# Strassen projections of a two-layer encoder: results held in PSUM, halves of q and k paired, weight sums on GpSimd

## The chip, the cores and the metric

The kernel runs on one core of one Trainium2 chip. Five engines share its SBUF: TensorE (PE, matrix products into PSUM, with PEld for its weight loads), VectorE (DVE), ScalarE (ACT), GpSimd (POOL) and SyncE (SP, which issues nearly all DMAs from one queue in order). The metric is the time of one execution on the device, in microseconds, of the slowest core, here the only one.

## The reference, cut to what matters

The trunk has two layers over a sequence of 2048 positions of width 1024. Layer 0 is a short gated convolution. Layer 1 is a dilated sliding-window attention with 8 heads of 128 and three groups (windows 128, 512, 2048 at rates 1, 4, 16). The change concerns the input projection of layer 1 and the rotation of q and k:

```python
h, gate = adaln_pre_norm(x, c, norm_g[i], w_mod[i], b_mod[i])     # (1, 2048, 1024)
q, k, v, z = jnp.split(h @ w_in, [G * E, 2 * G * E, 2 * G * E + E], axis=-1)   # 3072, 3072, 1024, 1024 columns
q = apply_rope(q.reshape(B, S, G, H, Dh), cos, sin)
k = apply_rope(k.reshape(B, S, G, H, Dh), cos, sin)

def apply_rope(x, cos, sin):
    x1, x2 = jnp.split(x.astype(jnp.float32), 2, axis=-1)
    return jnp.concatenate([x1 * cos - x2 * sin, x2 * cos + x1 * sin], axis=-1)
```

Behind it come banded attention in each group, a softmax over the three groups, `* silu(z)`, the output projection, the residual and a final RMSNorm.

## The kernel before, in words

All of it is one function, `build`, that issues instructions into pools of tiles; a scheduler then sets the order of each engine from the data's dependences and the pools' free buffers. Activations lie transposed: a tile holds 128 features by 512 positions (`CH`); the sequence has four such chunks (`NCH`).

Float32 products are made of three products of a reduced format: each operand is cut into a high and a low part (`cut`, `split`), and `hi*hi + hi*lo + lo*hi` is summed in PSUM.

Layer 0 ends with its output projection for chunks 2 and 3, which writes the residual stream `x1_d` and, between its matmuls, makes forms of the first half (`make_forms`, called with `c == 2`). `SumSq` gathers the sum of squares of a chunk for the norm; `ss.rstd()` sums over partitions with a matmul on PE into `ss` (L211) and takes the root (L152 to L157); the result goes to `r_d`.

The projections of layer 1 are the stretch that the change is about. They use Strassen's scheme (in Winograd's form) one level deep. The sequence is handled in two halves of two chunks each; the inner dimension is halved into k tiles 0 to 3 and 4 to 7; and two blocks of 128 output columns are one pair (`pair`). Seven products take the place of eight. The forms of the activations (`FN`: "11", "T2", "T3", "T1", "21", "22", "T4") are made once per half and lie in SBUF as `F`; the first four are in pool `fa`, the others in `fb`. The forms of the weights (`w_forms`) are made for every pair: two raw tiles `wraw` (512 KB each) are loaded, S1, S2, S3 and S4 (A12 - S2) are computed into tiles `st`, then each of the seven is cast on ACT (L529) and its low part subtracted (L425, in `sub`) into a tile `wf`, of which there are eight. A product (`prod`, L537) is 12 matmuls of 128 by 512; a pair is 84.

A half has 32 pairs (`jobs`): 4 for z, 4 for v, 24 for q and k, in this order. In a q/k pair the one block is the q and the other the k of a head and group. `pair` sums the products into four tiles `u` in SBUF (L541, L559) and hands each to `emit`:

- z: SiLU on ACT, then a store.
- v: four transposes on PE (L585), a copy out of PSUM, a store.
- q and k (`qk_out`): ACT copies the two 64-partition halves crosswise into `sw` (L603, L604), DVE multiplies by cos (L605), POOL multiplies `sw` by sin (L606), DVE adds both into `R`, in an order of positions that suits the group's rate (L607), and two stores go to `q_d` and `k_d` (L612).

At the turn between the halves (last pair of the first, first pair of the second) `pair` runs with `by_k`: it goes over the k tiles outside and the seven products inside, so that a k tile's forms can be replaced as soon as it is done (`load_forms`, through a ring of six tiles `fs`). The forms of the second half are made behind the pairs 8, 12, 16 and 20 of the first (the q/k pairs begin with 8) and kept in DRAM.

Behind the projections come the pools of the attention (`mk`, `qkp`), whose loads of q and k (`load_qk`, L668) stand on SP behind the last stores of `R`.

## Time and profile before

| what | us |
|---|---|
| median of 3 runs (lowest, highest) | 3091.41 (3088.41, 3094.56) |
| the profiled execution's own time | 3090.82 |
| its span, first to last instruction | 3089.0 |
| PE busy | 2816.2 |
| DVE busy | 2032.4 |
| POOL busy | 1410.9 |
| ACT busy | 1208.9 |

The engines run beside each other, so busy times don't add up to the span. [...] In the slices of the page PE and its clock are below their full marks from about 950 us to 1200 us, and again and again until 2450.

### The profile page before, as it was taken

Reading aid. Unit: us, or ns where it says so; the run is one execution under the profiler, and the core shown is the slowest. Engines: PE = TensorE matmul, PEld = TensorE weight load, DVE = VectorE, ACT = ScalarE, POOL = GpSimd, SP = SyncE. Lnnn points to the kernel's source line nnn. Section 1 sums busy time; section 2 is a strip of 40 time slices with the busy share of each in tenths; the row PEclk is TensorE's granted clock in tenths of the full one; section 3 lists DMA queues with packets and bytes.
Section 4 is the critical chain, followed back from the end, with each engine's and each line's share of the span. In section 5 each row is a group of like instructions: output and inputs, shape, how many; then the busy total and the mean of one; then the engine's idle time right before and its main releaser. Section 6 shows DMA issues by size and latency. Waiting matters only on the chain. (4 is left out here: it accounts for less than half of the span.)

```text
span 3089.0 us, 39549 instructions
## 1 busy us (share of the span) xinstructions
PE 2816.2 (91%) x13910; PEld 2372.2 (77%) x13910; DVE 2032.4 (66%) x3265; ACT 1208.9 (39%) x2599; POOL 1410.9 (46%) x1038
## 2 busy tenths in 40 slices
PE   5999997999997969998989699998989689999998
PEld 4999995888886758877777487877777578887888
...
GB/s 217 67 80 69 74 118 118 87 70 81 68 130 167 181 195 112 96 95 96 90 96 95 156 122 98 89 102 90 96 96 95 133 211 235 219 219 196 173 155 96
DMA packets 246694, 384.66 MB, mean 125 GB/s; under 512 B 89056, under 2 KB 146656, under 8 KB 238304
## 3 DMA queue, kind: packets, MB, share of 16 engines
...
## 5 line engine op out<-in xcount | busy, mean ns | idle before, releaser
L537 PE MATMUL mm<-fT,wf 128*128 128x512 f32 x3072 | 770.9, 407 | 105.4 <-DVE u L541 85.8
L537 PEld LDWEIGHTS mm<-fT,wf 128*128 128x128 f32 x3072 | 600.5, 197 | 257.0 <-ACT wf L529 112.5
L537 PE MATMUL mm<-f,wf 128*128 128x512 f32 x2304 | 561.3, 394 | 16.3 <-ACT u L559 6.9
L537 PEld LDWEIGHTS mm<-f,wf 128*128 128x128 f32 x2304 | 435.2, 190 | 109.8 <-ACT u L559 7.3
L127 POOL TENSOR_TENSOR wf<-wraw,wf 128x512 fp32r<-128x512 f32 x148 | 198.1, 1340 | 591.1 <-ACT wf L126 586.2
L606 POOL TENSOR_TENSOR sw<-sw,sin 128x512 f32<-128x512 f32 x192 | 348.7, 1816 | 162.8 <-ACT sw L604 162.8
L135 PE MATMUL mm<-hA,wf 128*128 128x342 f32 (+1 forms) x2304 | 369.8, 323 | 6.0 <-DVE hA L225 5.6
L135 PEld LDWEIGHTS mm<-hA,wf 128*128 128x128 f32 x2304 | 366.8, 191 | 7.6 <-DVE hA L225 6.5
L607 DVE TENSOR_TENSOR R<-u,sw 128x512 f32<-128x512 f32 x192 | 322.3, 1678 | 66.2 <-POOL sw L606 62.2
L135 PE MATMUL mm<-hB,wf 128*128 128x512 f32 x1536 | 351.6, 391 | 0.0
L135 PEld LDWEIGHTS mm<-hB,wf 128*128 128x128 f32 x1536 | 288.8, 188 | 61.4 <-issue 1.5
L425 POOL TENSOR_TENSOR wf<-st,wf 128x512 fp32r<-128x512 f32 x192 | 249.8, 1313 | 152.5 <-ACT wf L529 152.5
L541 DVE TENSOR_TENSOR u<-mm,u 128x512 f32<-128x512 f32 x384 | 256.8, 685 | 89.1 <-PE mm L537 72.9
L529 ACT CAST wf<-st 128x512 fp32r<-128x512 f32 x256 | 148.1, 618 | 335.9 <-DVE st L425 308.4
L605 DVE TENSOR_TENSOR u<-u,cos 128x512 f32<-128x512 f32 x192 | 233.0, 1214 | 67.3 <-ACT sw L604 67.3
L603 ACT COPY sw<-u 64x512 f32<-64x512 f32 x192 | 118.9, 619 | 324.5 <-DVE u L541 318.7
L811 PE MATMUL po<-ptS,v 128*128 128x128 f32 (+1 forms) x1280 | 199.0, 288 | 21.0 <-ACT ptS L794 8.4
L425 POOL TENSOR_TENSOR wf<-wraw,wf 128x512 fp32r<-128x512 f32 x128 | 170.5, 1332 | 85.1 <-ACT wf L529 83.8
L811 PEld LDWEIGHTS po<-ptS,v 128*128 128x128 f32 (+1 forms) x1280 | 165.4, 192 | 47.2 <-ACT ptS L794 13.3
L696 ACT ACTIVATE pr<-pr,stat 128x256 f32<-128x256 f32 (+2 forms) x384 | 173.6, 454 | 69.7 <-DVE stat L694 68.6
L692 PE MATMUL pq<-k,q 128*128 128x256 f32 (+2 forms) x768 | 169.0, 349 | 33.7 <-DMA k<-k_d 33.7
L135 PE MATMUL mm<-y,wf 128*128 128x512 f32 x768 | 180.4, 397 | 0.0
...
## 6 DMA issues: line engine op xcount, KB each, us to landing
...
```

What stands on the lines that cost most here:

```text
L127: e.tensor_tensor(out=t[:, 1], in0=part, in1=t[:, 0].bitcast(F32), op=ALU.subtract)
L135: PE.matmul(ps, lhs(l, kt), rhs(r, kt), start=start and i == 0 and j == 0, stop=stop and i == n - 1 and j == 2)
L425: eng.tensor_tensor(out=out, in0=in0, in1=in1, op=ALU.subtract)
L529: SC.copy(out=t[:, 0], in_=x)
L537: PE.matmul(ps, W[i][:, l, k, :], F[FN[i]][:, r, k, :], start=k == 0 and j == 0, stop=k == HK - 1 and j == 2)
L541: V.tensor_tensor(out=out, in0=in0, in1=in1, op=op)
L605: V.tensor_tensor(out=src, in0=src, in1=cos[:, cs], op=ALU.mult)
L606: G.tensor_tensor(out=sw, in0=sw, in1=sin[:, cs], op=ALU.mult)
L607: V.tensor_tensor(out=Rs[m].rearrange("p (r j) -> p j r", r=r)[:, t * n:(t + 1) * n, :], in0=src.rearrange("p (j r) -> p j r", r=r), in1=s ...
L692: PE.matmul(pq[:, j, 0:n], q[:, q0:q0 + P], k[:, k0:k0 + n], start=True, stop=True)
L696: SC.activation(out=pr[:, j, 0:n], in_=pr[:, j, 0:n], func=AF.Exp, scale=-1.0, bias=m_ap, accum_out=l_ap)
L811: PE.matmul(po[:, b % 4, :], vt[0:m, vc, :], ptS[0:m, i, :], start=ci == 0, stop=ci == len(parts) - 1)
```

## The change

The arithmetic of the seven products stays. What changes around them:

- **Blocks.** The columns of the q and k weights are put in another order on the host: a pair's first block holds the first 64 dimensions of q and of k, its second block the second 64 of both. `cos` and `sin` have the same values in both halves of the partitions. A rotation is then `A cos - B sin` and `B cos + A sin` of the two blocks, with no crossing of partitions; the crosswise copies and POOL's products go. A tile `R` now holds halves of q and k, and is stored with four DMAs of 64 partitions.
- **PSUM.** Four of the seven products become the results, in place: adds write the bank that they read. `u` is left for three partial sums x, y, z. DVE multiplies by sin into a tile `t` and by cos in place in PSUM, and the `R` sums read PSUM. z's SiLU reads PSUM; v is first copied to SBUF by ACT.
- **Weights.** All sums and low parts are on POOL, with their tiles `st` in a pool of their own (`stp`) that is there before the stage. `w_forms` of the next pair is issued before `pair` of this one.
- **Order and pools.** The first half runs z, q/k, v; the second z, v, q/k. The forms of the second half are made behind pairs 1 to 4. The sums of squares of chunks 2 and 3 are stored as they are (`r_d`), and the root is taken behind pair 0. The ring for forms (six tiles) and the two rows `r23` lie in q and k tiles of the attention's first buffer (`qk0`), which is there from the start of the stage; the second buffer is `qk1`.

```diff
+    stp = tc.alloc_tile_pool(name="stp", bufs=1, side="right")
...
-        ss = SumSq(op, CH)
+        ss = SumSq(op, CH, row=False)
...
-        SY.dma_start(out=r_d[c], in_=ss.rstd())
+        V.tensor_tensor(out=ss.acc, in0=ss.acc, in1=ss.sq, op=ALU.add)
+        SY.dma_start(out=r_d[c], in_=ss.acc)
...
+    qk0 = tc.alloc_tile_pool(name="qk0", bufs=1)
+    spare = [t[:, i * CH:(i + 1) * CH] for t in [qk0.tile([P, S], F32, name=n) for n in ("q", "k")] for i in range(4)]
+    r23 = spare[:2]
+    fring = itertools.cycle(spare[2:])
...
-        S1, S2, S3 = (l1.tile([P, HK, P], F32, name="st", bufs=4) for i in range(3))
+        S1, S2, S3 = (stp.tile([P, HK, P], F32, name="st", bufs=4) for i in range(3))
         G.tensor_tensor(out=S1, in0=A21, in1=A22, op=ALU.add)
-        sub(S2, S1, A11, V)
+        sub(S2, S1, A11, G)
...
-        for x, eng in ((A11, G), (S2, V), (S3, G), (S1, G), (A12, G), (None, G), (A22, V)):
+        for x, eng in ((A11, G), (S2, G), (S3, G), (S1, G), (A12, G), (None, G), (A22, G)):
...
-                sub(x, A12, S2, V)
+                sub(x, A12, S2, G)
...
-        SC.copy(out=c11, in_=product(0))
-        add(c12, product(1), c11)
-        add(c21, product(2), c12)
-        p5 = product(3)
-        add(c12, p5, c12)
-        add(c22, p5, c21)
+        p1 = product(0)
+        x, y, z = (l1.tile([P, CH], F32, name="u", bufs=4) for i in range(3))
+        SC.copy(out=x, in_=p1)
+        add(y, product(1), x)
+        add(z, product(2), y)
+        c22 = product(3)
+        add(y, c22, y)
+        add(c22, c22, z)
         emit(1, 1, c22)
-        add(c11, product(4), c11)
+        c11 = product(4)
+        add(c11, c11, x)
         emit(0, 0, c11)
-        add(c12, product(5), c12)
+        c12 = product(5)
+        add(c12, c12, y)
         emit(0, 1, c12)
-        add(c21, c21, product(6), ALU.subtract)
+        c21 = product(6)
+        add(c21, z, c21, ALU.subtract)
         emit(1, 0, c21)
...
         def emit(m, t, src):
-            cs = slice(t * CH, (t + 1) * CH)
-            sw = l1.tile([P, CH], F32, name="sw", bufs=2)
-            SC.copy(out=sw[0:64], in_=src[64:128])
-            SC.copy(out=sw[64:128], in_=src[0:64])
-            V.tensor_tensor(out=src, in0=src, in1=cos[:, cs], op=ALU.mult)
-            G.tensor_tensor(out=sw, in0=sw, in1=sin[:, cs], op=ALU.mult)
-            V.tensor_tensor(out=Rs[m].rearrange("p (r j) -> p j r", r=r)[:, t * n:(t + 1) * n, :],
-                            in0=src.rearrange("p (j r) -> p j r", r=r),
-                            in1=sw.rearrange("p (j r) -> p j r", r=r), op=ALU.add)
...
+            s_ = t_tile()
+            mul(s_, src, sin, t)
+            mul(src, src, cos, t)
+            got[m, t] = src, s_
+            if (1 - m, t) not in got:
+                return
+            done.append(t)
+            for i in range(2):
+                V.tensor_tensor(out=Rs[i].rearrange("p (r j) -> p j r", r=r)[:, t * n:(t + 1) * n, :],
+                                in0=got[i, t][0].rearrange("p (j r) -> p j r", r=r),
+                                in1=got[1 - i, t][1].rearrange("p (j r) -> p j r", r=r),
+                                op=ALU.add if i else ALU.subtract)
...
+    jobs = [(half, *j) for half in range(2) for j in ((zj + qj + vj) if half == 0 else (zj + vj + qj))]
...
+    Wn = w_forms(*jobs[0][1:3])
+    load_forms(0)
+    for i, (half, s0, s1, what, args) in enumerate(jobs):
+        W = Wn
+        if i + 1 < len(jobs):
+            Wn = w_forms(*jobs[i + 1][1:3])
+        if i == NJ:
+            load_forms(1)
...
+        pair(W, what(half, *args), i in (NJ - 1, NJ))
...
+        if 1 <= i <= 4:
+            make_forms(lambda: next(fring), 1, i - 1, r23, store_form(1))
...
-            qk[hd, g] = [qkp.tile([P, S], F32, name=n) for n in ("q", "k")]
+            qk[hd, g] = [(qk1 if (hd * NG + g) % 2 else qk0).tile([P, S], F32, name=n) for n in ("q", "k")]
```

The scheduler moves work at three places that matter here. The names in the rows are those of the tiles; a line of the kernel after stands some lines later than before.

First, DVE in a q/k pair. Before, from the end of one pair into the next (`u` and `R` in SBUF, `sw` from POOL, `st`, `wraw` and `wf` the weights):

```order
L607 TENSOR_TENSOR R1_11332<-u_11335,sw_11455 128x512
L425 TENSOR_TENSOR st_11631<-st_11630,wraw_11626 128x512
L425 TENSOR_TENSOR st_11651<-wraw_11626,st_11631 128x512
L425 TENSOR_TENSOR wf_11639<-st_11631,wf_11639 128x512
L541 TENSOR_TENSOR u_11498<-mm_11515,u_11497 128x512
L541 TENSOR_TENSOR u_11499<-mm_11529,u_11498 128x512
L541 TENSOR_TENSOR u_11498<-mm_11543,u_11498 128x512
L541 TENSOR_TENSOR u_11500<-mm_11543,u_11499 128x512
L605 TENSOR_TENSOR u_11500<-u_11500,cos_8071 128x512
L541 TENSOR_TENSOR u_11497<-mm_11564,u_11497 128x512
L607 TENSOR_TENSOR R1_11496<-u_11500,sw_11558 128x128x4
L605 TENSOR_TENSOR u_11497<-u_11497,cos_8071 128x512
```

After, from a pair's first add on (`mm` is a PSUM bank, `t` the product with sin):

```order
L544 TENSOR_TENSOR u_10891<-mm_10894,u_10890 128x512
L544 TENSOR_TENSOR u_10892<-mm_10908,u_10891 128x512
L544 TENSOR_TENSOR u_10891<-mm_10922,u_10891 128x512
L544 TENSOR_TENSOR mm_10922<-mm_10922,u_10892 128x512
L612 TENSOR_TENSOR t_10937<-mm_10922,sin_7403 128x512
L612 TENSOR_TENSOR mm_10922<-mm_10922,cos_7402 128x512
L544 TENSOR_TENSOR mm_10940<-mm_10940,u_10890 128x512
L612 TENSOR_TENSOR t_10954<-mm_10940,sin_7403 128x512
L612 TENSOR_TENSOR mm_10940<-mm_10940,cos_7402 128x512
L544 TENSOR_TENSOR mm_10957<-mm_10957,u_10891 128x512
L612 TENSOR_TENSOR t_10971<-mm_10957,sin_7403 128x512
L612 TENSOR_TENSOR mm_10957<-mm_10957,cos_7402 128x512
```

The weight operations have left DVE, a result is written back to its bank, and each product follows its add directly, without `sw` between.

Second, POOL at the start of the projections (`f_7408` and `f_7396` are the form "21", `fT` is a form with T in its name; `q` and `k` in the rows after are tiles of the ring). Before, from the first pair's sums on:

```order
L520 TENSOR_TENSOR st<-wraw 128x512
L425 TENSOR_TENSOR st<-wraw 128x512
L425 TENSOR_TENSOR wf<-st,wf 128x512 x2
L425 TENSOR_TENSOR wf<-wraw,wf 128x512
L425 TENSOR_TENSOR wf<-st,wf 128x512
L425 TENSOR_TENSOR f_7408<-fs,f_7408 128x512 x4
L425 TENSOR_TENSOR wf<-wraw,wf 128x512
L425 TENSOR_TENSOR fT_7410<-fs,fT_7410 128x512 x4
L520 TENSOR_TENSOR st<-wraw 128x512
```

After, from the second pair's sums on:

```order
L523 TENSOR_TENSOR st<-wraw 128x512
L426 TENSOR_TENSOR st<-st,wraw 128x512
L426 TENSOR_TENSOR st<-wraw 128x512
L426 TENSOR_TENSOR st<-wraw,st 128x512
L426 TENSOR_TENSOR f_7396<-q,f_7396 128x512
L426 TENSOR_TENSOR wf<-st,wf 128x512
L426 TENSOR_TENSOR f_7396<-q,f_7396 128x512
L426 TENSOR_TENSOR wf<-st,wf 128x512
L426 TENSOR_TENSOR f_7396<-k,f_7396 128x512 x2
L426 TENSOR_TENSOR wf<-st,wf 128x512
L426 TENSOR_TENSOR fT_7398<-k,fT_7398 128x512
L426 TENSOR_TENSOR wf<-wraw,wf 128x512
```

The four sums of the second pair's weights, and two low parts, now stand ahead of or between the cuts of "21"; before, four cuts of "21" followed the low parts of the first pair's weights.

Third, POOL at the turn between the halves. Before, from a sum for the second half's first pair on:

```order
L425 TENSOR_TENSOR st<-wraw 128x512
L425 TENSOR_TENSOR f_7408<-fs,f_7408 128x512
L425 TENSOR_TENSOR fT_7410<-fs,fT_7410 128x512
L425 TENSOR_TENSOR f_6619<-fs,f_6619 128x512
L425 TENSOR_TENSOR fT_6621<-fs,fT_6621 128x512
L425 TENSOR_TENSOR f_7408<-fs,f_7408 128x512
L425 TENSOR_TENSOR fT_7410<-fs,fT_7410 128x512
L425 TENSOR_TENSOR f_6619<-fs,f_6619 128x512
L425 TENSOR_TENSOR wf<-st,wf 128x512 x2
L425 TENSOR_TENSOR wf<-wraw,wf 128x512
```

After, from the last sum for that pair on:

```order
L426 TENSOR_TENSOR st<-wraw,st 128x512
L426 TENSOR_TENSOR fT_6624<-k,fT_6624 128x512
L426 TENSOR_TENSOR f_7396<-q,f_7396 128x512
L426 TENSOR_TENSOR fT_7398<-k,fT_7398 128x512
L426 TENSOR_TENSOR f_6622<-k,f_6622 128x512
L426 TENSOR_TENSOR fT_6624<-k,fT_6624 128x512
L426 TENSOR_TENSOR f_7396<-q,f_7396 128x512
L426 TENSOR_TENSOR fT_7398<-k,fT_7398 128x512
L426 TENSOR_TENSOR f_6622<-k,f_6622 128x512
L426 TENSOR_TENSOR fT_6624<-q,fT_6624 128x512
L426 TENSOR_TENSOR f_7396<-k,f_7396 128x512
L426 TENSOR_TENSOR wf<-st,wf 128x512 x3
```

Six low parts of the weights stand behind the cuts of forms, as before; there are ten cuts between the last sum and the first of these low parts, and no sums of others.

## Rows read from the trace of the kernel before

**Rows 1.** part 1 of the page: busy us, share of the span, instructions of each engine
```profile
PE 2816.2 (91%) x13910; PEld 2372.2 (77%) x13910; DVE 2032.4 (66%) x3265; ACT 1208.9 (39%) x2599; POOL 1410.9 (46%) x1038
```

**Rows 2.** stretches: length, busy PE, PEld, DVE, ACT, POOL, PEclk, DMA share, GB/s
```profile
992.50:1209.00 216.50, 177.28 (x746) 138.79 (x745) 117.50 (x135) 73.76 (x126) 105.00 (x80) 0.91 0.53 166
1209.00:1701.80 492.80, 455.53 (x1926) 370.07 (x1925) 421.45 (x419) 211.99 (x354) 378.39 (x244) 0.97 0.30 94
1701.80:1781.30 79.50, 54.11 (x182) 38.56 (x181) 67.07 (x61) 40.07 (x70) 64.96 (x43) 0.81 0.48 146
1781.30:1924.40 143.10, 143.10 (x653) 115.39 (x652) 58.72 (x77) 50.46 (x85) 66.16 (x52) 1.00 0.38 116
1924.40:2438.10 513.70, 475.38 (x2005) 385.58 (x2003) 439.54 (x439) 220.74 (x368) 388.76 (x252) 0.97 0.29 92
```

**Rows 3.** timeline of PE, second half: start, us, engine, line, instruction, count
```profile
1781.29 8.32 PE L537 MATMUL mm<-fT,wf 128*128 128x512 f32 x36
...
1800.33 8.32 PE L537 MATMUL mm<-fT,wf 128*128 128x512 f32 x36
...
1859.93 8.33 PE L537 MATMUL mm<-fT,wf 128*128 128x512 f32 x36
...
1881.39 8.33 PE L537 MATMUL mm<-fT,wf 128*128 128x512 f32 x36
```

**Rows 4.** groups, second q/k stretch: line, count | busy us, mean ns | idle before
```profile
L606 POOL TENSOR_TENSOR sw<-sw,sin 128x512 f32<-128x512 f32 x92 | 167.2, 1818 | 77.1 <-ACT sw L604 77.1
...
L607 DVE TENSOR_TENSOR R<-u,sw 128x512 f32<-128x512 f32 x92 | 153.9, 1673 | 31.8 <-POOL sw L606 29.9
L605 DVE TENSOR_TENSOR u<-u,cos 128x512 f32<-128x512 f32 x92 | 112.2, 1220 | 32.9 <-ACT sw L604 32.9
L541 DVE TENSOR_TENSOR u<-mm,u 128x512 f32<-128x512 f32 x140 | 93.9, 685 | 8.5 <-PE mm L537 3.8
L425 POOL TENSOR_TENSOR wf<-st,wf 128x512 fp32r<-128x512 f32 x69 | 88.0, 1288 | 43.3 <-ACT wf L529 43.3
...
L529 ACT CAST wf<-st 128x512 fp32r<-128x512 f32 x92 | 52.7, 618 | 128.5 <-DVE st L425 125.4 <-PE mm L537 2.4
...
L425 DVE TENSOR_TENSOR st<-st,wraw 128x512 f32<-128x512 f32 x23 | 40.1, 1742 | 2.6 <-POOL st L520 2.6
```

**Rows 5.** waits, second q/k stretch: total us, times, longest us
```profile
PEld mm L537 <- ACT wf L529: 45.8, 19, 3.6
...
PE mm L537 <- DVE u L541: 38.3, 19, 3.2
```

**Rows 6.** timeline within a q/k pair of the first half
```profile
1422.69 1.78 DVE L607 TENSOR_TENSOR R<-u,sw 128x512 f32<-128x512 f32 x1 [0.59 <-POOL sw L606]
...
1426.69 0.67 DVE L607 TENSOR_TENSOR R<-u,sw 128x512 f32<-128x512 f32 x1
...
1428.18 1.80 POOL L606 TENSOR_TENSOR sw<-sw,sin 128x512 f32<-128x512 f32 x1 [2.57 <-ACT sw L604]
```

**Rows 7.** timeline around the start of the projections
```profile
947.55 2.08 PE L211 MATMUL ss<-acc,ones 128*128 128x512 f32 x2 [8.15 <-DVE acc L204]
...
948.64 43.99 PE L135 MATMUL mm<-y,wf 128*128 128x512 f32 x182
...
1009.18 1.22 PE L537 MATMUL mm<-fT,wf 128*128 128x512 f32 x2 [12.67 <-ACT wf L529]
```

**Rows 8.** timeline around the end of the projections
```profile
2450.79 1.03 DVE L607 TENSOR_TENSOR R<-u,sw 128x512 f32<-128x512 f32 x1
...
2452.41 1.09 SPq L668 DMA_DIRECT2D q<-q_d  x1
...
2462.37 12.91 PE L692 MATMUL pq<-k,q 128*128 128x192 f32 x56 [24.28 <-DMA k<-k_d]
```

**Rows 9.** tile wraw, 1300 to 1700 us: its loads
```profile
DMA to landing us min/median/max: 3.3/3.5/4.1
```

**Rows 10.** groups of POOL, z and v pairs of the second half
```profile
L425 POOL TENSOR_TENSOR wf<-wraw,wf 128x512 fp32r<-128x512 f32 x15 | 19.3, 1287 | 42.9 <-ACT wf L529 41.5 <-DVE u L541 1.3
```

More of the change, by code (lines that the diff above doesn't have):

```diff
@@ L425, in sub @@
         eng.tensor_tensor(out=out, in0=in0, in1=in1, op=ALU.subtract)
-    def fs_tile(pool, bufs):
-        return pool.tile([P, CH], F32, name="fs", bufs=bufs)
     def cut(n, k, x, eng=V):
@@ L433, in cut, with make_forms @@
         sub(F[n][:, 1, k, :], x, hi.bitcast(F32), eng)
-    def make_forms(pool, bufs, half, k, rs, use):
+    def make_forms(fs_tile, half, k, rs, use):
         def h(c, kt):
-            x = fs_tile(pool, bufs)
+            x = fs_tile()
             SY.dma_start(out=x, in_=x1_d[2 * half + c][:, kt, :])
@@ L582, in emit @@
         def emit(m, t, src):
+            vs = t_tile()
+            SC.copy(out=vs, in_=src)
             pt = ps_s.tile([P, CH], F32, name="ss")
             for q in range(4):
-                PE.transpose(out=pt[:, q * P:(q + 1) * P], in_=src[:, q * P:(q + 1) * P], identity=ident)
-            vt = l1.tile([P, 4, P], F32, name="sw", bufs=2)
+                PE.transpose(out=pt[:, q * P:(q + 1) * P], in_=vs[:, q * P:(q + 1) * P], identity=ident)
+            vt = l1.tile([P, H2], F32, name=f"R{m}", bufs=1)[:, 0:CH].rearrange("p (t e) -> p t e", t=4)
             SC.copy(out=vt.rearrange("p t e -> p (t e)"), in_=pt)
@@ L615, in qk_out @@
-        return emit
-    jobs = [(a["wz"][2 * p], a["wz"][2 * p + 1], z_out, (p,)) for p in range(4)]
-    jobs += [(a["wv"][2 * p], a["wv"][2 * p + 1], v_out, (p,)) for p in range(4)]
-    jobs += [(a["wqk"][2 * i], a["wqk"][2 * i + 1], qk_out, divmod(i, NG)) for i in range(NG * NH)]
-    for half in range(2):
-        for i, (s0, s1, what, args) in enumerate(jobs):
-            W = w_forms(s0, s1)
-            if i == 0:
-                load_forms(half)
-            if i == 4:
-                cos = l1.tile([P, H2], F32, name="cos", bufs=1)
-                sin = l1.tile([P, H2], F32, name="sin", bufs=1)
-                SY.dma_start(out=cos, in_=a["cos"][:, half * H2:(half + 1) * H2])
-                SY.dma_start(out=sin, in_=a["sin"][:, half * H2:(half + 1) * H2])
-            pair(W, what(half, *args), (half, i) in ((0, len(jobs) - 1), (1, 0)))
-            if half == 0 and i == 8:
-                r23 = [l1.tile([P, CH], F32, name=f"r{c}", bufs=1) for c in (2, 3)]
-                for c in range(2):
-                    SY.dma_start(out=r23[c], in_=r_d[2 + c])
-            if half == 0 and 8 <= i < 24 and i % 4 == 0:
-                make_forms(l1, FSB, 1, i // 4 - 2, r23, store_form(1))
@@ new lines, in emit @@
+            if len(done) == 2:
+                for i in range(2):
+                    R = Rs[i].rearrange("p (r j) -> p r j", r=r)
+                    for d, x in ((q_d, R[0:64]), (k_d, R[64:128])):
+                        SY.dma_start(out=d[hd][g][64 * i:64 * i + 64].rearrange("p (r j) -> p r j", r=r)
+                                     [:, :, half * 2 * n:(half + 1) * 2 * n], in_=x)
+        return emit
+    zj = [(a["wz"][2 * p], a["wz"][2 * p + 1], z_out, (p,)) for p in range(4)]
+    vj = [(a["wv"][2 * p], a["wv"][2 * p + 1], v_out, (p,)) for p in range(4)]
@@ new lines, in build, with trig @@
+    qj = [(a["wqk"][2 * i], a["wqk"][2 * i + 1], qk_out, divmod(i, NG)) for i in range(NG * NH)]
+    jobs = [(half, *j) for half in range(2) for j in ((zj + qj + vj) if half == 0 else (zj + vj + qj))]
+    NJ = len(jobs) // 2
+    cos = l1.tile([P, H2], F32, name="cos", bufs=1)
+    sin = l1.tile([P, H2], F32, name="sin", bufs=1)
+    def trig(half):
+        SY.dma_start(out=cos, in_=a["cos"][:, half * H2:(half + 1) * H2])
+        SY.dma_start(out=sin, in_=a["sin"][:, half * H2:(half + 1) * H2])
@@ new lines, in build @@
+    Wn = w_forms(*jobs[0][1:3])
[6 more added lines that the diff above has]
+            load_forms(1)
+        if i % NJ == 2:
+            trig(half)
+        pair(W, what(half, *args), i in (NJ - 1, NJ))
+        if i == 0:
+            for c in range(2):
+                acc, var = next(fring), next(fring)
+                SY.dma_start(out=acc, in_=r_d[2 + c])
+                ps = ps_s.tile([P, CH], F32, name="ss")
+                PE.matmul(ps, ones, acc, start=True, stop=True)
+                rstd_row(ps, var, r23[c])
+        if 1 <= i <= 4:
+            make_forms(lambda: next(fring), 1, i - 1, r23, store_form(1))
@@ L644, in build @@
     fa.release()
+    stp.release()
     wp.release()
```

42 lines of the change are left out of this document (20 added, 22 removed).

## The prediction

> **What bounds the kernel now.** I read the engines' busy times first. PE is busy for 2816.2 of 3089.0 us [rows 1], so a gain has to come from stretches in which PE is not at its pace. The clean pace is in the timeline of PE: in the z pairs of the second half one pair (84 matmuls, `pair`) follows another after 19.04 us (1781.29 to 1800.33), and a v pair, with 16 transposes more, after 21.46 us (1859.93 to 1881.39) [rows 3]. Cutting the projections (992.5 to 2438.1 us, 1445.6 us, 64 pairs) at the changes of job gives the reader three kinds of stretch [rows 2]:
> - z and v of the second half, 1781.3 to 1924.4: PE 143.10 of 143.10 us, clock 1.00. Nothing to gain.
> - the two q/k stretches, 492.8 and 513.7 us: PE 92%, clock 0.97, DVE 86%. The second holds 24 pairs, 21.40 us each, so 2.36 us a pair are lost; the first holds about 23 pairs at 21.4.
> - three broken stretches: the start with the first half's z and v (216.5 us, where 8 x 19.04 + 4 x 2.42 = 162 would do, 54 lost), and the turn between the halves (79.5 us for two pairs, 41 lost).
>
> In the second q/k stretch the waits of PE end on DVE's `u` and on ACT's `wf` [rows 5]. Both are DVE's: it adds the products late, and it makes S2 and S4 late, which ACT casts. The groups say why DVE is late: 92 cos products at 1220 ns and 92 `R` sums at 1673 ns, where adds that read a product from PSUM take 685 [rows 4]. The same line takes 1.78 us at one time and 0.67 at another, when POOL stands still (2.57 us before 1428.18) [rows 6]. Per pair DVE has 4 x 1.22 + 4 x 1.67 + 7 x 0.685 + 1.74 for S2 and three more weight operations at some 0.69, 20.2 us of work, in order, and PE needs only 19.04.
>
> **The change part by part.** Sums are against the profiled execution's 3090.82 us (span 3089.0), which is 0.6 us under the median of 3091.41.
>
> *DVE in a q/k pair.* The four weight operations go to POOL, the 8 half-copies of ACT (L603, L604) go away, and the products of sin come from POOL. What is left: 7 adds, 8 products, 4 `R` sums, 19 instructions, each with one input in PSUM. At 0.685 for 15 of them and 1.03 for a strided `R` sum alone [rows 8] that is 10.3 + 4.1 = 14.4 us, against 19.04. Eight of them write PSUM in place, which no row shows on DVE. Bounds: 0.67 us (an SBUF form alone; no two-input row of 512 columns read here is shorter) and 1.78 us (the contended form) [rows 6]. I take 0.685, the row with a PSUM operand, since the output only replaces an SBUF one. At 1.78, with the `R` sums as today, the pair has 8 x 1.78 + 7 x 0.685 + 4 x 1.67 = 25.7 us.
>
> *POOL in a pair.* It loses 4 x 1.818 us of sin products [rows 4] and gets S2, S4 and two low parts: 11 instructions. Beside DVE's PSUM adds one takes 1.287 us [rows 10], so 14.2 us. POOL works a pair ahead; its raw weights have two buffers, both held by one pair, so a cycle is 14.2 + a landing of 3.5 us [rows 9] = 17.7 us and the time of two issues, still under 19.04 (the first of the two tiles comes free two instructions earlier). The eight `wf` slots let tile i of the next pair be filled once product i-1 of this one is done, so the last is ready some 18 us into the pair and needed 17 us later: POOL may be late by about 9 us before PE sees it. On SP each pair's four `R` stores stand behind the weight loads of two pairs ahead, which come free first; nothing is blocked.
>
> *PSUM.* Results stay in their banks until the rotation is done. The first half's c22 is freed about 4 us after product 5; its bank is wanted again 8 us into the next pair. Seven banks are enough at no cost; if DVE were 7 us late this cover would be gone.
>
> So the 64 pairs at PE's pace: 64 x 19.04 = 1218.6 us, transposes 8 x 2.42 = 19.4, the two moved `ss` matmuls 1.1.
>
> *Extras, stretch by stretch.* Start: today PE idles 12.67 us behind a cast of the first weights [rows 7], whose sums lie in `l1`, a pool that needs the space of `op` and so waits until its last store has landed. With `stp` the first weights are made under the stage before. But POOL then has the next pair's four sums ahead of the four cuts of "21" (second piece of the order): from about 7 us after the start 11 instructions of 1.29 run until 16, "21" is wanted from 10.9, T4 is done at about 24 instead of 19. I take 5 lost; bounds 0 and today's 13. Forms of the second half (`make_forms`) now fall into pairs 1 to 4, with 8 DVE operations of up to 1.78 us (14 us, beside 4.8 us of adds): 18.9 us fills a pair, and a six-tile ring makes POOL wait for loads. 6 lost; bounds 0 and 41, which is today's 54 less the start's 13. Turn: PE's order by k needs all seven tiles `wf` in the first 4.8 us, while POOL has 11 cuts of forms and three sums ahead of six of them (third piece of the order): some 14 x 1.5 = 21 us from 5 us into the last pair, so the tiles come about 9 to 11 us late. The pair in front is now v, with little left on DVE. 14 lost; bounds 5 and today's 41. v: each transpose now waits for an ACT copy more, 0.62 us by the cast of that size [rows 4], and stands about 3 matmuls (0.7 us) later. 5 lost; bounds 0 and 32 x 0.6 = 19. Together 30, bounds 5 and 114; no bound is below nothing, as PE has no faster pace in any row.
>
> Projections after: 1218.6 + 19.4 + 1.1 + 30 = 1269, today 1445.6: **-176 us**.
>
> *Before them.* The row sums of chunk 2 leave PE's order: PE waited 8.15 us for `acc`, and the next 182 matmuls took 43.99 us instead of 41.3 at the full pace [rows 7]. Gain 8.15 + 1.1 (to 948.64) + 2.7 = 12; I take 10, as banks can still run short behind DVE's forms.
>
> *Behind them.* Today DVE, ACT and POOL need from 2438.1 to 2451.8 us for the last pair, then the loads of q and k take 9.96 us (2452.41 to 2462.37), and PE idles 24.28 [rows 8]. Now after the last product: add, two products, two `R` sums (3 x 0.685 + 2 x 1.03 = 4.1 us), some 1.1 us for the last two stores, and the same load: 15.2 instead of 24.3 us. Gain **9**. The two loads of `wo` that now stand in front of the last stores go out in the idle time before them. The attention behind has the same order of work and is costed at nothing.
>
> Sum: 3090.8 - 176 - 10 - 9 = 2896; I round to **2900**, as the small terms lean to the slow side.
>
> **Rivals.**
> - *In-place PSUM work is dear.* Place: DVE in the 48 q/k pairs. At 1.78 us for the eight PSUM outputs and 1.67 for the `R` sums a pair takes 25.7 us and DVE binds: 48 x (25.7 - 19.04) = +320, 3220 us, slower than before. It decides from 1.45 us an instruction on (the 195 us of gain over 48 pairs are 4.06, so a pair of 23.1 us loses them: 23.1 - 4.8 - 6.7 = 11.6 for eight). Against it: the adds with a PSUM input take 685 ns, an SBUF form alone 670 [rows 4, 6]. [...]
> - *The weight chain binds.* With landings of 4.1 us [rows 9], a cast of 0.62 us waited for, 0.7 for two issues and 14.7 for the sums (a tenth of them slowed to 1.8), a cycle is 20.1 us: 64 x 1.1 = +70, 2970 us. For it: only two raw tiles. Against it: the first is free early.
> - *The broken stretches stay as they are*: 54 + 41 instead of 25: +70, 2970 us. For it: POOL's order at start and turn; a six-tile ring as before. Against it: DVE no longer shares these with rotation.
> - *The pairs don't get shorter*, because ACT's casts in order wait on POOL instead of DVE: 48 x 2.36 = +113, 3013 us. For it: 45.8 us of PE's waits end on `wf` today. Against it: a pair of lead.
>
> **How the numbers follow.** Forecast 66%; weight chain 10%; broken stretches 15%; pairs as before 5%; PSUM dear 4%. Its own range comes from the extras: 5 instead of 30 and the 2 us kept at chunk 2 take 2896 to 2869, and some 25 more than taken give 2925. To leave out no more than two in ten it must take in the two cases near 2970: 2868 to 2970. A measurement of this kernel tells 0.2% (6 us) from no change. Faster 0.94, within 0.02, slower 0.04.
>
> **What would show it.** Right: q/k stretches at 19.0 to 19.3 us a pair with clock 1.00, no PE wait on DVE in them; DVE's products and `R` sums at 0.68 and 1.03 us; POOL's subtractions at 1.29 us with some idle time on the landing of `wraw`; a start without the 12.7 us, a turn under 60 us, a gap of 15 us before attention. Wrong: PE waiting on `wf` once a pair, DVE instructions on PSUM above 1.3 us, or a turn as long as today's 79.5 us.

## The result, and the profile after

The changed kernel takes 2937.45 us (median of four runs, 2935.74 to 2938.02), beside 3092.66 us for the kernel before: a ratio of 0.9499, 95% interval [0.9483, 0.9515]. The forecast was 2900, the range 2868 to 2970. So the gain is 155 us where 191 were forecast. The profiled execution has a span of 2934.0 us, and answers to [rows 1] so:

```profile
PE 2767.5 (94%) x13910; PEld 2353.9 (80%) x13910; DVE 1696.7 (58%) x3201; ACT 998.6 (34%) x2247; POOL 1347.4 (46%) x1102
```

The projections now run from 982.4 to 2288.4 us, 1305.9 us instead of 1445.6. Cut into stretches as in [rows 2] (first pair; pairs 1 to 5; the first half's q/k pairs; its v pairs and the turn, that is pairs 28 to 32; the rest of the second half's z pairs, its v pairs and its first q/k pair; the other 23 q/k pairs):

```profile
982.40:1025.50 43.10, 28.93 (x86) 19.84 (x86) 19.68 (x21) 18.52 (x33) 38.41 (x29) 0.72 0.60 186
1025.50:1148.50 123.00, 103.45 (x424) 82.94 (x423) 84.34 (x96) 38.20 (x65) 85.99 (x63) 0.92 0.58 194
1148.50:1567.40 418.90, 418.90 (x1849) 346.85 (x1848) 291.87 (x419) 108.37 (x176) 310.73 (x245) 1.00 0.40 112
1567.40:1687.30 119.90, 107.66 (x486) 86.53 (x485) 38.67 (x51) 57.06 (x100) 88.16 (x68) 0.96 0.46 141
1687.30:1850.30 163.00, 160.87 (x738) 131.32 (x737) 43.89 (x66) 64.60 (x113) 115.75 (x92) 1.00 0.35 107
1850.30:2288.40 438.10, 438.07 (x1933) 362.42 (x1931) 304.21 (x438) 110.66 (x178) 307.72 (x242) 1.00 0.38 107
```

Third and last row: PE is busy throughout at a clock of 1.00; 22 and 23 q/k pairs take 19.04 and 19.05 us each, and the 21.40 of before are gone. What is missing against the forecast is in the first two rows: the first pair takes 43.1 us, and the granted clock there is 0.72, a mean over stretches at 1.00 (from 997 to 1001 us) and, after waits of PE, at 0.50 (from 990 to 994 and from 1003.4 to 1018 us).

The groups of DVE in the second q/k stretch (1900 to 2200 us) answer to [rows 4]; a line, its count, busy us, mean ns, idle before:

```profile
L623 DVE TENSOR_TENSOR R<-mm,t 128x512 f32<-128x512 f32 x64 | 56.0, 942 | 0.0
L612 DVE TENSOR_TENSOR t<-mm,sin 128x512 f32<-128x512 f32 x64 | 44.3, 692 | 2.2
L612 DVE TENSOR_TENSOR mm<-mm,cos 128x512 f32<-128x512 f32 x64 | 44.1, 689 | 0.0
L544 DVE TENSOR_TENSOR mm<-mm,u 128x512 f32<-128x512 f32 x48 | 33.4, 696 | 12.5 <-PE mm L540 11.0
L544 DVE TENSOR_TENSOR u<-mm,u 128x512 f32<-128x512 f32 x47 | 32.5, 692 | 77.1 <-PE mm L540 77.1
```

An instruction that writes PSUM in place costs 0.69 us, what one with a PSUM input costs (the subtraction that ends a pair, a group not shown, 0.73), and the idle time of DVE now ends on PE: DVE waits for products, where PE waited for DVE [rows 5]. POOL, in the same stretch:

```profile
L426 POOL TENSOR_TENSOR wf<-wraw,wf 128x512 fp32r<-128x512 f32 x48 | 62.3, 1298 | 45.0 <-ACT wf L532 45.0
```

To compare the runs that follow, each projection stage is cut at the starts of products in PE's timeline. The stretches between (1148.5 to 1567.4 and 1850.3 to the last product here) are at the pace in every run but one, and left out. "Gap" is from the last product to the first score of the attention. The column "z, v" holds one q/k pair too. Us:

| kernel | median | first pair | pairs 1-5 | v, turn | z, v | gap |
|---|---|---|---|---|---|---|
| the pace alone | | 19.0 | 95.2 | 95.2 + 9.7 | 152.3 + 9.7 | |
| changed | 2937.45 | 43.1 | 123.0 | 119.9 | 163.0 | 18.4 |
| e2 weights on both engines | 2915.51 | 39.3 | 115.2 | 115.8 | 160.4 | 18.2 |
| e3 no lead | 2933.24 | 44.8 | 119.1 | 118.3 | 166.5 | 18.4 |
| e4 forms off GpSimd | 2929.87 | 45.0 | 116.4 | 120.8 | 165.0 | 18.0 |
| e5 forms' loads first | 2935.51 | 33.3 | 132.3 | 121.3 | 163.8 | 18.0 |
| e6 cuts on DVE | 2928.06 | 39.9 | 122.8 | 114.4 | 164.6 | 18.1 |
| e7 early q and k | 2929.33 | 43.6 | 126.1 | 122.6 | 164.6 | 5.0 |
| e8 rotation in PSUM alone | 2909.45 | 37.3 | 111.7 | 115.5 | 160.3 | 18.0 |
| e10 together | 2896.13 | 35.6 | 116.1 | 110.2 | 160.4 | 5.0 |
| e11 together, loads first | 2909.76 | 34.0 | 129.0 | 109.6 | 160.6 | 5.0 |
| e12 together, last set late | 2892.21 | 35.2 | 103.0 | 119.0 | 160.4 | 5.0 |

Each row is one profiled execution. Where the order of the work is the same (e7 up to the turn, and e9 below), a stretch repeats within some 3 us, so a smaller difference of one stretch tells nothing by itself.

### The profile page after: what moved, and what is told of

Read it like the earlier page. It is cut to its first block, busy times and chain, and to the rows that moved or that the text cites. A ratio compares the mean times of both kernels' runs of the same rounds, so it can differ in the third digit from the quotient of the medians.

```text
span 2934.0 us, 38626 instructions
## 1 busy us (share of the span) xinstructions
PE 2767.5 (94%) x13910; PEld 2353.9 (80%) x13910; DVE 1696.7 (58%) x3201; ACT 998.6 (34%) x2247; POOL 1347.4 (46%) x1102
## 5 line engine op out<-in xcount | busy, mean ns | idle before, releaser
L540 PE MATMUL mm<-fT,wf 128*128 128x512 f32 x3072 | 734.9, 394 | 23.9 <-DVE R L623 11.5
L540 PEld LDWEIGHTS mm<-fT,wf 128*128 128x128 f32 x3072 | 582.6, 190 | 149.4 <-issue 11.9
L127 POOL TENSOR_TENSOR wf<-wraw,wf 128x512 fp32r<-128x512 f32 x148 | 197.5, 1337 | 580.8 <-ACT wf L126 578.8
L426 POOL TENSOR_TENSOR wf<-st,wf 128x512 fp32r<-128x512 f32 x256 | 331.6, 1318 | 72.8 <-ACT wf L532 72.8
L426 POOL TENSOR_TENSOR wf<-wraw,wf 128x512 fp32r<-128x512 f32 x192 | 251.9, 1312 | 179.9 <-ACT wf L532 179.8
L544 DVE TENSOR_TENSOR u<-mm,u 128x512 f32<-128x512 f32 x192 | 132.7, 691 | 339.0 <-PE mm L540 267.9
L532 ACT CAST wf<-st 128x512 fp32r<-128x512 f32 x256 | 157.7, 621 | 354.9 <-POOL st L426 212.0
L532 ACT CAST wf<-wraw 128x512 fp32r<-128x512 f32 x192 | 119.3, 621 | 353.6 <-PE mm L540 297.1
L544 DVE TENSOR_TENSOR mm<-mm,u 128x512 f32<-128x512 f32 x192 | 133.1, 695 | 80.1 <-PE mm L540 75.9
L623 DVE TENSOR_TENSOR R<-mm,t 128x512 f32<-128x512 f32 x192 | 170.6, 957 | 0.0
L135 PEld LDWEIGHTS mm<-y,wf 128*128 128x128 f32 x768 | 145.1, 189 | 31.6 <-issue 1.5
```

The source lines that it names most:

```text
L127: e.tensor_tensor(out=t[:, 1], in0=part, in1=t[:, 0].bitcast(F32), op=ALU.subtract)
L135: PE.matmul(ps, lhs(l, kt), rhs(r, kt), start=start and i == 0 and j == 0, stop=stop and i == n - 1 and j == 2)
L426: eng.tensor_tensor(out=out, in0=in0, in1=in1, op=ALU.subtract)
L532: SC.copy(out=t[:, 0], in_=x)
L540: PE.matmul(ps, W[i][:, l, k, :], F[FN[i]][:, r, k, :], start=k == 0 and j == 0, stop=k == HK - 1 and j == 2)
L544: V.tensor_tensor(out=out, in0=in0, in1=in1, op=op)
```

## The experiments

**e1, results in SBUF.** In the second half's q/k pairs alone:

```diff
-        c22 = product(3)
-        add(y, c22, y)
-        add(c22, c22, z)
+        def res(p):
+            return next(fring) if sbuf else p
+
+        p5 = product(3)
+        c22 = res(p5)
+        add(y, p5, y)
+        add(c22, p5, z)
...
-        pair(W, what(half, *args), i in (NJ - 1, NJ))
+        pair(W, what(half, *args), i in (NJ - 1, NJ), half == 1 and what is qk_out)
```

and so for the other three results (`fring` is the ring of six tiles for forms).

> The changed kernel, but in the 24 q/k pairs of the second half the four results of a pair are written to SBUF tiles and rotated from there; the first half's pairs keep them in PSUM and are the control. Theory (what makes the pairs short is that DVE's 19 instructions each have an operand in PSUM, so they do not slow down beside GpSimd): in the second half the eight products rise from 0.69 to about 1.2 us and the R sums from 0.96 to about 1.67, DVE needs 7 x 0.69 + 8 x 1.2 + 4 x 1.67 = 21.1 us, a pair takes 21.3 to 21.5 us, and the time rises by some 24 x 2.4 = 55 us to about 2990. Rival (DVE simply has fewer instructions, where the operands lie does not matter): products stay at 0.69, pairs at 19.04, time 2937 within 6.

Measured: 2984.86 us, ratio to the kernel before 0.9647 [0.9624, 0.967], 47 us over the changed kernel. The first half keeps 19.04 us a pair; in the second, 15 pairs from 1969.57 to 2290.42 us take 21.39 each. DVE's groups there, as above:

```profile
L630 DVE TENSOR_TENSOR R<-k,t 128x512 f32<-128x512 f32 x38 | 74.4, 1997 | 0.0
L619 DVE TENSOR_TENSOR k<-k,cos 128x512 f32<-128x512 f32 x37 | 48.1, 1299 | 1.3
L619 DVE TENSOR_TENSOR t<-k,sin 128x512 f32<-128x512 f32 x37 | 39.5, 1068 | 1.3
L544 DVE TENSOR_TENSOR u<-mm,u 128x512 f32<-128x512 f32 x42 | 28.8, 686 | 3.3 <-DVE u L544 0.5
```

These are the groups whose ring tile lies in `k`; where it lies in `q` the same products take 1.06 and 1.21 us and the sums 1.83. So the same instructions, on the same tables, take 1.06 to 1.30 us instead of 0.69 where both inputs lie in SBUF, with POOL busy for 253.0 of 300 us (1970 to 2270), and the sums 1.83 to 2.0 instead of 0.94; the adds, which read PSUM, stay at 0.69. DVE is busy for 292.9 of the 300 us there. GpSimd is slowed too: its groups take 1.51 to 1.89 us, in the changed kernel 1.29 to 1.30:

```profile
L426 POOL TENSOR_TENSOR wf<-st,wf 128x512 fp32r<-128x512 f32 x56 | 92.7, 1674 | 0.0
```

It is not the number of instructions but the place of one operand that made the pairs short.

**e2, part of the weights back on DVE.**

```diff
-        sub(S2, S1, A11, G)
+        sub(S2, S1, A11, V)
...
-        for x, eng in ((A11, G), (S2, G), (S3, G), (S1, G), (A12, G), (None, G), (A22, G)):
+        for x, eng in ((A11, G), (S2, V), (S3, G), (S1, G), (A12, G), (None, G), (A22, V)):
...
-                sub(x, A12, S2, G)
+                sub(x, A12, S2, V)
```

> The changed kernel with S2, S4 and the low parts of tiles 2 and 7 back on DVE, as before the change. Theory (DVE had no room for them): 14.4 us of rotation and adds, two sums of 1.74 and two low parts of 1.3 make 20.5 us a q/k pair; the 48 pairs take 20.5 to 21.0 instead of 19.04 us, +70 to +90 us, about 3015. Rival (with the rotation in PSUM DVE has room: 14.4 + 4 x 0.69 = 17.2 us, under 19.04): q/k pairs stay at 19.04, and the start and the turn, where GpSimd is late, gain up to 10 us: 2927 to 2940.

Measured: 2915.51, ratio 0.942 [0.9401, 0.9439]: 22 us faster than the changed kernel, more than the rival had it; the theory falls. The window of a q/k stretch (1900 to 2200), and two of the four groups:

```profile
1900.00:2200.00 300.00, 300.00 (x1325) 248.42 (x1324) 249.90 (x365) 76.31 (x127) 147.77 (x110) 1.00 0.39 111
```

```profile
L426 DVE TENSOR_TENSOR st<-st,wraw 128x512 f32<-128x512 f32 x16 | 13.6, 851 | 0.0
L426 DVE TENSOR_TENSOR wf<-wraw,wf 128x512 fp32r<-128x512 f32 x16 | 11.1, 693 | 0.0
```

DVE is busy for 249.90 of 300 us, 15.9 a pair, and the pair stays at 19.04. With the rotation in PSUM and POOL at 49% the four operations cost 0.68 to 0.85 us, where [rows 4] have 1.74 for the first of them. All four broken stretches get shorter. In the first two it is POOL's lateness: PE's waits on its `wf` of 2.65 us in the first pair and 3.65 and 2.31 in pairs 4 and 5 are 0.49, 0.42 and 1.97 here, on DVE's. PE's wait for DVE in pair 5, 11.49 us in the changed kernel (shown at e4), halves as well:

```profile
1120.89 4.61 PE L540 MATMUL mm<-fT,wf 128*128 128x512 f32 x10 [5.76 <-DVE R L623]
```

**e3, no lead.** The weights of a pair are made with the pair:

```diff
-        W = Wn
-        if i + 1 < len(jobs):
-            Wn = w_forms(*jobs[i + 1][1:3])
+        W = w_forms(s0, s1)
```

> The changed kernel with the weight sums of a pair issued with the pair itself instead of one pair ahead. Theory (the eight tiles wf set the lead: a tile can only be filled when a product of the pair before has freed it, so in the middle of a stretch the order on GpSimd is the same): q/k pairs stay at 19.04 us, and only the pairs at the start and at the change of stage move; time within 12 us of 2937. Rival (the lead is what took PE's waits for wf away): q/k pairs return to 21.4 us, 48 x 2.36 = +113, 3050.

Measured: 2933.24, ratio 0.9479 [0.9457, 0.9501], q/k pairs at 19.04. Not told from the changed kernel: the lead is worth nothing that can be measured. In pairs 4 and 5 the waits change places: the one for DVE is gone, and one of 6.21 us for ACT's `wf` stands there.

**e4, forms without GpSimd's multiplications,** in `make_forms`:

```diff
-            if kt % 2 == 0:
+            if half or kt % 2 == 0:
```

> The changed kernel, with the second half's forms scaled by DVE and ScalarE only: the eight GpSimd multiplications of pairs 2 and 4 (the odd k) go away, DVE keeps as many instructions. Theory (DVE stands 13.9 us behind a form's instruction that waits for GpSimd's multiplication, which stands behind the weights there; the pair's adds are queued behind it, and PE waits 11.49 us for a bank): the 11.49 us wait goes, the stretch from 1029.7 to 1140.4 us gets 12 us shorter, about 2925. Rival (DVE is simply full in these pairs, with up to 14 us of forms beside 15 us of rotation and adds): the wait stays within 3 us, 2937 within 4.

Measured: 2929.87, ratio 0.9464 [0.9442, 0.9486]. The chain in the changed kernel is in these rows of its timeline:

```profile
1111.13 1.29 POOL L523 TENSOR_TENSOR st<-wraw 128x512 f32<-128x512 f32 x1 [6.33 <-DMA wraw<-in_wqk]
...
1118.70 1.27 POOL L444 TENSOR_TENSOR q<-q 128x512 f32<-128x512 f32 x1
1119.93 1.27 POOL L444 TENSOR_TENSOR k<-k,q 128x512 f32<-128x512 f32 x1
1120.00 1.48 DVE L445 TENSOR_SCALAR q<-q,amul,mod 128x512 f32<-128x512 f32 x1 [13.90 <-POOL q L444]
...
1135.94 1.62 PE L540 MATMUL mm<-fT,wf 128*128 128x512 f32 x3 [11.49 <-DVE R L623]
```

POOL comes late to the multiplications because it has first waited 6.33 us for raw weights and then made sums and low parts of the next pair. In e4 PE's wait is 5.06 us instead of 11.49 (11.38, 11.02 and 11.48 in e5, e6 and e7, which leave the multiplications), and pairs 1 to 5 are 6.6 us shorter: half of what the theory had. By the time alone e4 is hardly told from the changed kernel, the intervals touch. The other half was left open, and e12 takes it up.

**e5, the forms' loads first.** In `load_forms`, and for the two raw weights of pair 1 in the same way:

```diff
-            SY.dma_start(out=x, in_=f_d[half][n][:, k, :])
+            d = SY.dma_start(out=x, in_=f_d[half][n][:, k, :])
+            if half == 0:
+                tc.keep_in_program_order(d)
```

> The changed kernel with one order pinned on the DMA queue: at the start of the projections the loads of the forms 21, 22 and T4 come ahead of the two loads of the second pair's raw weights, behind which they stand now (issued at 994.5 and 997.0, when GpSimd frees those buffers; the forms' loads follow at 997.4, though their space is free when PE ends the stage before, at 982.4). Theory (this order makes the first pair late): the forms' loads go out from 982.5, PE's wait of 2.66 us on the cast of f goes and the GpSimd cuts start some 8 us earlier; the first pair takes 33 to 36 us instead of 43.1, about 2929. Rival (what was predicted: GpSimd has its weight work ahead of the cuts whatever the queue does): the first pair stays within 3 us of 43.1; the second pair can even be later, since its raw weights now come last: 2935 to 2945.

Measured: 2935.51, ratio 0.949 [0.9476, 0.9504]. The queue in the changed kernel, and in e5:

```profile
994.48 0.33 SPq L519 DMA_DIRECT2D wraw<-in_wz  x1
...
996.96 0.33 SPq L520 DMA_DIRECT2D wraw<-in_wz  x1
997.38 0.86 SPq L514 DMA_DIRECT2D q<-f_d  x2
```

```profile
986.41 0.89 SPq L514 DMA_DIRECT2D q<-f_d  x2
...
1011.34 1.17 PE L665 MATMUL ss<-q,ones 128*128 128x512 f32 x2 [2.57 <-DMA q<-r_d]
...
1067.82 8.48 PE L542 MATMUL mm<-f,wf 128*128 128x512 f32 x24 [3.87 <-ACT t L588]
...
1131.51 2.90 PE L542 MATMUL mm<-fT,wf 128*128 128x512 f32 x6 [11.38 <-DVE R L625]
```

The first pair is 9.8 us shorter, as the theory said, and pairs 1 to 5 are 9.3 longer. New waits of 2.57 us for a load and 3.87 for ACT stand there, with slower matmuls behind them (24 take 8.48 us, 5.4 at the pace), and the wait for DVE is as long as before: it ends 152.9 us after the stage's start, in the changed kernel 153.5. A local theory was right and the gain was nil, because what ends that wait did not come earlier.

**e6, all low parts of loaded forms on DVE.**

```diff
-            cut(n, k, x, V if FN.index(n) % 2 else G)
+            cut(n, k, x, V)
```

> The changed kernel with all low parts of loaded forms made by DVE, eight of which at the start and sixteen at the turn were GpSimd's. Theory (GpSimd is the late engine there): the waits on GpSimd's f at the start (4.16, 1.25, 1.71, 0.26, 0.28 us) go, while the wait for the load, 2.66 us, stays: the first pair 36 instead of 43.1 us; the turn, where PE waits 6.89 us behind a copy that stands behind the casts of late loads, some 4 us shorter since the six load tiles come free earlier; about 2926. Rival (the loads set the pace in both places): 2935 to 2940.

Measured: 2928.06, ratio 0.9466 [0.9452, 0.9481]. The first pair gains 3 us, not 7 (the waits move to ACT's `f`), which is no more than a repetition differs by, the turn 5.5. There PE waits for a bank behind a copy of ACT, first in the changed kernel, then in e6:

```profile
1658.05 1.65 PE L540 MATMUL mm<-f,wf 128*128 128x512 f32 x3 [6.89 <-ACT u L563]
```

```profile
1649.19 1.53 PE L540 MATMUL mm<-f,wf 128*128 128x512 f32 x3 [3.33 <-ACT u L563]
```

**e7, early q and k,** ahead of the last `pair` instead of in `load_qk`:

```diff
+        if i == len(jobs) - 1:
+            qk[0, 0] = [qk0.tile([P, S], F32, name=n) for n in ("q", "k")]
+            SY.dma_start(out=qk[0, 0][0], in_=q_d[0][0])
+            SY.dma_start(out=qk[0, 0][1], in_=k_d[0][0])
```

> The changed kernel with the first q and k of attention loaded ahead of the last pair instead of behind its last four stores. Theory (the gap of 18.4 us is the 4 us of DVE's last rotation, 4 us in which the queue issues four stores of 0.5 to 1.4 us and 10.4 us of the load): the first score follows when DVE has freed the banks, some 5 us after the last product, a gap of 5 to 8 us, 10 to 13 us shorter: about 2926. Rival (the scores' results, pr, lie where the last rotation's R tiles lie, and the second pair of q and k waits as before, so that the time comes back as 2.4 and 7.5 us waits that grow): gap shorter, time 2933 to 2938.

Measured: 2929.33, ratio 0.9468 [0.9452, 0.9483]. The gap falls from 18.4 to 5.0 us, and a later load takes over:

```profile
2298.00 8.62 PE L728 MATMUL pq<-k,q 128*128 128x192 f32 x32 [4.97 <-issue]
2311.50 0.72 PE L728 MATMUL pq<-k,q 128*128 128x192 f32 x2 [4.89 <-DMA k<-k_d]
```

From the last product to the end of the span e7 takes 640.0 us and the changed kernel 645.6. So 5.6 of the 13.4 us remain.

**e8, the rotation in PSUM alone:** e2 and e3 together.

> Only the rotation in PSUM and the pools of the change: S2, S4 and two low parts on DVE as in the kernel before, and no lead of the weights. Theory (the whole gain is the rotation's; the work moved to GpSimd cost about 20 us and the lead nothing): 2908 to 2918, q/k pairs at 19.04 us. Rival (with DVE making part of the weights the lead is needed): q/k pairs above 19.5 us, 2940 or more.

Measured: 2909.45, ratio 0.9407 [0.9393, 0.9421], q/k pairs at 19.04. The rotation in PSUM, with the pools and orders around it, gives 184 us; the moved weight work and the lead take 28 of them back. How the 184 divide between the rotation and the new order and pools was not run; e1 prices the place of the results alone, 47 us for half of the q/k pairs. Pairs 1 to 5, with all four sets of forms beside them, have no wait for DVE's `R` here; the longest in pairs 4 and 5 is this:

```profile
1107.69 0.73 PE L540 MATMUL mm<-f,wf 128*128 128x512 f32 x2 [2.18 <-ACT wf L532]
```

**e9, e10, e11.** e9 is the changed kernel with this edit, e10 is e8 with it and those of e6 and e7, and e11 is e10 with the order of e5.

```diff
-        if 1 <= i <= 4:
-            make_forms(lambda: next(fring), 1, i - 1, r23, store_form(1))
+        if i in (1, 2, 3, NJ - 4):
+            make_forms(lambda: next(fring), 1, min(i, 4) - 1, r23, store_form(1))
```

> The changed kernel, with the last of the four sets of forms made beside the first v pair (pair 28) instead of beside pair 4, the first q/k pair. Theory (a set of forms beside a q/k pair's rotation is what DVE cannot take: PE waits 11.4 us for a bank there, with and without the earlier start of the experiment before): the pairs 4 and 5 run at 19.0 to 24 us, the waits of 2.3 and 11.5 us go, the stage gets 13 to 17 us shorter; a v pair has 4.9 us of adds on DVE and takes the set at a cost under 3 us: about 2923. Rival (the set is late wherever it stands, since its loads and GpSimd's multiplications hold DVE up): the 11 us turn up at pair 28 or at the turn, 2935 to 2940.

> The parts that gained put together: the rotation in PSUM, weights made as in the kernel before and without a lead (2909.5), the last set of forms in the first v pair, all low parts of loaded forms on DVE, the first q and k of attention loaded early. Theory (these places are apart, so their gains add: 5 to 12 us of forms, 5 us at the turn and 3 at the start, 6 at the tail): 2888 to 2897. Rival (what is gained in one place is waited for in the next, as the earlier start was): 2903 to 2910.

> The same with the forms' loads pinned ahead of the second pair's raw weights at the start. Theory (the 9.8 us that this gained in the first pair were given back beside the last set of forms, which DVE and GpSimd now have off their hands): first pair 30 to 33 us, and 5 to 9 us less than without the pin, 2880 to 2890. Rival (they are given back at the second and third pair, whose raw weights are loaded later): within 3 us of the kernel without the pin.

e9 tested nothing: the scheduler put the set of forms back where it stood, and the orders on PE and GpSimd are those of the changed kernel. Its 2937.48 us, ratio 0.9495 [0.9478, 0.9512], are a repetition. e10: 2896.13, ratio 0.9361 [0.9343, 0.9379], 13 us under e8, at the upper edge of what the theory had. But its first term, 5 to 12 us of forms, was not tested here either, as the set still stood beside pair 4; the others (3, 5 and 6 us) give some 2895. Against e8 the turn is 5.3 us shorter and the gap 13.0, and pairs 1 to 5 are 4.4 longer. e11: 2909.76, ratio 0.9405 [0.9386, 0.9423], 14 us slower than e10, which neither theory nor rival had. Its first pair gains 1.6 us, and the second waits for weights whose loads now come last:

```profile
1028.93 1.22 PE L542 MATMUL mm<-fT,wf 128*128 128x512 f32 x2 [9.41 <-ACT wf L534]
```

**e12, the last set truly late:** e10, with this in `make_forms`, and the same for the stores of the first half's q/k pairs, ahead of which the loads may then not go:

```diff
-            SY.dma_start(out=x, in_=x1_d[2 * half + c][:, kt, :])
+            d = SY.dma_start(out=x, in_=x1_d[2 * half + c][:, kt, :])
+            if half and k == HK - 1:
+                tc.keep_in_program_order(d)
```

> The kernel of all gaining parts together (2896.1), with the loads of the last set of forms pinned on the DMA queue behind the stores of the first half's last q/k pair. In the two runs before, moving the set in the program to the first v pair did nothing, since the scheduler put DVE's instructions of the set back to where they stood; now they stand beside the v pairs. Theory (a set of forms, in DVE's order ahead of the pairs' adds and waiting for loads and GpSimd, is what holds the first q/k pairs up by waits of 1.6 and 8.4 us): those waits go, pairs 4 to 6 run at 19.0 to 20.5 us, the v pair loses under 3 us: 2884 to 2889. Rival (DVE is late from the sets before, and this set only stands where it shows): a wait over 5 us stays in pairs 4 to 6, or it returns beside the v pairs and at the turn: 2893 to 2900.

Measured: 2892.21 (five runs), ratio 0.9341 [0.9324, 0.9358]; its interval overlaps that of e10, and it is the lowest of all. In the trace the two waits of e10

```profile
1107.59 3.00 PE L540 MATMUL mm<-fT,wf 128*128 128x512 f32 x12 [1.63 <-DVE u L544]
...
1119.00 2.47 PE L540 MATMUL mm<-fT,wf 128*128 128x512 f32 x5 [8.41 <-DVE R L623]
```

are gone, pairs 1 to 5 are 13 us shorter, and beside the v pairs 8.8 come back, behind a wait like this:

```profile
1577.24 1.12 PE L598 MATMUL ss<-ident,t 128*128 128x128 f32 x4 [4.16 <-ACT t L595]
```

So both had a part: the set was what held the first q/k pairs of e10 up, and it costs most of that beside the v pairs too, where DVE's order again has it waiting for loads and POOL ahead of a pair's adds. It is not the set as such: e3 and e8 have it beside pair 4 and no such wait for DVE. It is where the set's instructions stand among the adds in DVE's order; what makes the scheduler put them there is open.

## Why the prediction was right, and where it was off

- *DVE in a q/k pair, 14.4 us.* Right: 209.6 us of DVE in 300 us of that stretch are 13.3 a pair. The value taken for in-place work (0.685, bounds 0.67 and 1.78) measured 0.689 to 0.730; the `R` sums 0.94 for 1.03. The rival of dear PSUM work falls, and e1 shows what the upper bound was: the price of two SBUF inputs beside a busy GpSimd (0.69 us with one SBUF input, 1.06 to 1.30 with two, POOL busy for 253.0 of 300 us; 0.67 with two where POOL stands still [rows 6]).
- *POOL in a pair, 14.2 us, in time at 19.04.* Right in the long stretches: 307.7 us in 438.1, 13.4 a pair, and no wait of PE. But the step took for granted that DVE had to be rid of the four operations. With the prediction's own durations (1.74 and three of 0.69) a q/k pair of DVE would have had 14.4 + 3.8 = 18.2 us, under 19.04, and the change itself shortens the 1.74 (0.85 in e2, with POOL busy for 49% of the time, 76% in the last of [rows 2]); e2 shows 15.9. It counted POOL's order at the start and the turn, but not against a version that leaves the four on DVE, which is 22 us faster. One of these operations takes DVE 0.68 to 0.85 us in e2, and POOL 1.29 to 1.30 in the changed kernel.
- *PE's pace, 19.04 us; the stage before, -10.* Right: the long stretches run at 19.04 and 19.05, and the stage starts at 982.44 instead of 992.46.
- *The start, 5 us lost, bounds 0 and 13.* The step that failed: 43.1 less 19.0 are 24 us, nearly five times the value taken and over its upper bound. The waits:

```profile
986.50 0.73 PE L540 MATMUL mm<-fT,wf 128*128 128x512 f32 x2 [1.18 <-ACT wf L532]
989.88 10.83 PE L540 MATMUL mm<-fT,wf 128*128 128x512 f32 x34 [2.65 <-POOL wf L426]
1003.38 0.80 PE L540 MATMUL mm<-f,wf 128*128 128x512 f32 x1 [2.66 <-ACT f L431]
1008.34 1.65 PE L540 MATMUL mm<-f,wf 128*128 128x512 f32 x3 [4.16 <-POOL f L426]
1011.25 1.65 PE L540 MATMUL mm<-f,wf 128*128 128x512 f32 x3 [1.25 <-POOL f L426]
1014.61 6.61 PE L540 MATMUL mm<-f,wf 128*128 128x512 f32 x17 [1.71 <-POOL f L426]
```

  With two of 0.3 they are 14.2 us; most of the other 10 is PE at a lower clock after them (0.50 from 990 to 994 us and from 1003.4 to 1018; 34 matmuls behind the wait of 2.65 us take 10.83 us, 7.7 at the pace). POOL's order, which the prediction counted, is in the 4.16 us; but it went wrong in four things. Its sum: eleven instructions of 1.29 us from 7 us on end at 21, not at 16. Its start: the first weights were not made under the stage before. The second raw tile was asked for at 978.83, when DVE had done with its buffer, so that POOL's sums began with the stage, and those of the second pair 19.6 us into it instead of 7, with the cuts of "21" behind them:

```profile
978.83 0.46 SPq L520 DMA_DIRECT2D wraw<-in_wz  x1
...
982.53 1.47 POOL L523 TENSOR_TENSOR st<-wraw 128x512 f32<-128x512 f32 x1
...
1002.01 1.26 POOL L523 TENSOR_TENSOR st<-wraw 128x512 f32<-128x512 f32 x1 [1.40 <-DMA wraw<-in_wz]
...
1007.02 1.26 POOL L426 TENSOR_TENSOR f<-q,f 128x512 fp32r<-128x512 f32 x1
```

  The queue: the forms' loads stood behind two loads of raw weights that wait for POOL (9.8 us of this pair, e5). And the matmuls after the waits, slower than the pace (by 3.1 us for the 34).
- *Forms in pairs 1 to 4, 6 us, bounds 0 and 41.* 123.0 less 95.2 and some 1 us of moved `ss` matmuls: 27, inside the bounds, over four times the value taken. It put every set of forms beside the 4.8 us of a z pair's adds, but pair 4, behind which the last set is issued, and pair 5 are q/k pairs: 14 and 14.4 us of DVE are 28, over 19.04. And it missed what DVE waits for: in order, one form instruction stood 13.9 us behind GpSimd (e4), with the pair's adds queued behind it. With DVE that late the cover in PSUM, which the prediction gave up at 7 us, was gone: PE's 11.49 us are a wait for a bank.
- *Turn 14, v 5.* The two stretches take 282.9 us, 247.5 at the pace and 19.4 of transposes: 16 us lost for 19 taken. That POOL's cuts have a part in it, as predicted, e6 shows: without them the stretch is 5.5 us shorter. But PE's longest wait there, 6.89 us, ends on ACT's copy out of a bank, not on the late `wf` that the prediction had, so that the size came out better than the mechanism.
- *The tail, -9.* It gave 5.9. DVE ends 4.9 us after the last product (4.1 taken), the load takes 10.4 (9.96), but the last stores keep the queue for longer than the 1.1 us taken:

```profile
2292.41 0.52 SPq L631 DMA_DIRECT2D q_d<-R  x1
2292.98 0.66 SPq L631 DMA_DIRECT2D k_d<-R  x1
2293.73 1.10 SPq L631 DMA_DIRECT2D q_d<-R  x1
2294.89 1.39 SPq L631 DMA_DIRECT2D k_d<-R  x1
2296.33 1.30 SPq L699 DMA_DIRECT2D q<-q_d  x1
```

Of the stage's 37 us over the forecast of 1269, the first six pairs account for 40: 52 us lost there where 12 were taken. Of the rivals, "the broken stretches stay" came true for the first stretch and not for the turn. "The weight chain binds" came true only where POOL also cuts or scales forms. The range held because it reached to those two, which is luck in part: neither happened as a whole, and its own range of 2869 to 2925, from the terms of the sum, would have missed 2937.
